# A weight tile's low part made in pieces of 256 columns on GpSimd instead of one of up to 1024

## The chip, the cores and the metric

The kernel runs on one core of a Trainium2 chip. The metric is the device time of one execution in microseconds; lower is better. The engines are named as in the profile: PE multiplies matrices (PEld are its weight loads), DVE, ACT and POOL (GpSimd) work elementwise, SP issues the transfers.

## What is computed

Two layers of a decoder over 1024 tokens of width 1024. In each, three groups of attention heads run side by side on the same normed input; then come a SwiGLU network and a gated embedding.

```python
for i in range(DEPTH):                      # DEPTH = 2
    proj = rms_norm(h, attn_norm[i]) @ w_in[i]          # 1024 x 2664
    # 6 heads: softmax attention from two low-rank projections (mla_w_uq, mla_w_ukv)
    # 5 heads: softmax over the 256 keys that an indexer scores highest, for each query
    # 5 heads: stick-breaking attention (cumulated log-sigmoids)
    h = h + mix @ w_o[i]
    hf = rms_norm(h, ffn_norm[i])
    h = h + (silu(hf @ w_gate[i]) * (hf @ w_up[i])) @ w_down[i]     # width 2816
    g = sigmoid(rms_norm(h, ple_norm[i]) @ w_ple_gate[i])
    h = h + g * (p[i] @ w_ple_proj[i])
return rms_norm(h, final_norm)
```

## The kernel before

The residual is held features by tokens, in two halves of 512 tokens. The program runs a dense part (in-projection, output projection, SwiGLU, embedding) of one half while the attention of another half runs beside it: `weave` mixes the two streams in one order for PE, which is written out by hand. On the other engines a scheduler with a model of durations orders what is ready.

**The weights.** To keep the accuracy of float32, each weight tile is split in two parts of a shorter type. `load_cols` fetches a tile of 128 rows, `kt` k tiles and some columns (mostly 8 k tiles of 128 columns, or 4 of 256 for `w_down`: 1024 columns a partition) into `wr`, which has three buffers. `split_w` copies it on ACT into the high part `wh` (L185) and subtracts that from it on POOL into the low part `wl` (L186). `wh` and `wl` have two buffers each. `gemm` then runs three matmuls for each k tile: high weights with the high and the low activations (L256, L257), low weights with the high ones (L258). For one of the weights (`mla_w_ukv`) columns change places, and the split goes k tile by k tile, in pieces of 256 columns.

**Others on POOL.** L881 multiplies the two factors of the stick-breaking weights, which PE then transposes (L818). L609 scales the gate of the SwiGLU. L313 adds up squares for the norms.

**Others on DVE.** The norms make the low part of the scaled activations (L302). The SwiGLU has L608 on the gate and L623 for the low part of the product, L572 adds the down projection. Queries are split at L750, keys and values at L283. L826 makes the low part of the transposed attention weights from PSUM; L878 is the scan of the stick-breaking heads. The 256 highest keys are found by a bit search that runs in the background of the attention: for each of 31 bits it makes a candidate (`cand`, L1084), counts the scores above it with one operation for each of two or four query tiles (`junk`, L1072), and then takes the bit or not (`inc`, L1086, and `key`, L1087), each of the three on 2 or 4 columns. `inc`, `key` and the next `cand` depend on each other in this order.

```python
            DVE.scalar_tensor_tensor(cand, key, 1 << b, xm, op0=ALU.bitwise_or, op1=ALU.bitwise_xor)
            yield from count(cand.bitcast(F32), ALU.is_ge)
            DVE.tensor_scalar(inc, cnt, float(TOPK), float(1 << b), op0=ALU.is_ge, op1=ALU.mult)
            DVE.tensor_tensor(key, key, inc, op=ALU.bitwise_or)
```

Of the kernel before, what the change touches and what calls it, by code (L numbers as in the profile page):

```python
# [13 lines left out]
ALU = mybir.AluOpType  # L14
AX = mybir.AxisListType

T = 1024
# [9 lines left out]
TOPK = 256  # L27
# [17 lines left out]
CUT = 3  # L45
VAL_AT = 6
# [12 lines left out]
def f32(ap):  # L59
    return ap.bitcast(F32)  # L60


def weave(main, side, main_total, side_total, finished, clock):
    """Traces a part of two streams together: side advances with main, at the pace that gets it through side_total
    as main ends, and in any case until finished(). Each yields what its piece weighs; side yields None while it
    waits for something that main has yet to trace."""
# [21 lines left out]
def trunk(ctx: ExitStack, tc, x, p, w_in, attn_norm, mla_q_norm, mla_w_uq, mla_kv_norm, mla_w_ukv,  # L88
# [35 lines left out]
    def spare_tile(m):  # L124
        """Where attention had tiles that it no longer needs."""
# [15 lines left out]
    # ---------------------------------------------------------------- constants  # L141
# [33 lines left out]
    # ---------------------------------------------------------------- the residual's first half  # L175
    # ---------------------------------------------------------------- helpers of the dense part
    def split_w(raw, hi, lo, *order):
        """Parts of raw; order: the views of a k tile between which its columns change places."""
        if order:
            read, write = order  # L180
            parts = [(read(raw[:, k]), write(hi[:, k]), write(lo[:, k])) for k in range(raw.shape[1])]
        else:
            parts = [(raw, hi, lo)]
        for a, h, l in parts:
            ACT.copy(h, a)  # L185
            POOL.tensor_tensor(l, a, f32(h), op=ALU.subtract)  # L186
        return hi, lo

    def load_cols(segs, kt, *order):
        """Weight columns as [128 (k), kt, sum of widths], split in two float32r parts."""  # L190
# [45 lines left out]
    def after(n, f):  # L236
        """TensorE's part of something, once n more k tiles' products have been traced."""
# [11 lines left out]
    def gemm(ps, w, act, ks, m0=0, first=True, last=True):  # L249
        """ps[m, tokens] (+)= w^T act over the k tiles ks, in three passes that keep float32's accuracy."""  # L250
# [12 lines left out]
    def gemm_pair(x, y, act, ks, cut):  # L263
        """Two products; the first one's last k tile comes after some of the second one's."""
# [9 lines left out]
    def priority(by):  # L274
        """Ahead (by < 0) or behind in the order in which free engines pick what is ready."""
# [9 lines left out]
    class Norm:  # L285
        """rms_norm over n feature tiles that come one at a time, as float32r parts of src * gain in res; what they
# [1003 lines left out]
```

## Time and profile before

| | |
|---|---|
| time, median of 3 runs | 3304.84 us (3303.76 to 3309.46) |
| span of the profiled execution | 3305.8 us, 1.0 us over the median |
| mean granted clock of PE | 0.978 of 2.4 GHz |
| PE busy | 3101.8 us, 94% |
| DVE busy | 2404.7 us, 73% |
| ACT busy | 1484.6 us, 45% |
| POOL busy | 1378.0 us, 42%, of it 1046.1 in L186 |
| transfers | 363.50 MB, mean 110 GB/s |

The first table of the profile gives the busy time of each engine. A view by stretches of the span gives the same for parts of it, with the granted clock. The chain that ended last is followed back from the last instruction, at each step to what released it or to the one before it on its engine; its shares say whose time the end hangs on. The views by line give count, busy time, mean duration, and what ended the idle time before. A timeline has the instructions in order of time.

### The profile page before, as it was taken

The numbers are of one execution on the slowest core, as the hardware profiler recorded it, in microseconds if no ns is written. First come the engines' busy times: TensorE is split into PE (matmuls) and PEld (weight loads), VectorE is DVE, ScalarE is ACT, GpSimd is POOL, SyncE is SP. The second block draws the span as 40 slices with busy tenths as digits, with TensorE's granted clock in tenths as the row PEclk, the third lists the DMA queues.
The fourth block names the chain that finished last, engine by engine and source line by source line (L and its number), as shares of the span: only waits on it lengthen the run. The fifth ranks groups of instructions, "written<-read, shape, count | busy, mean of one in ns | idle before, by whom it ended". The sixth has DMA issues, their size and how long they took to land.

```text
span 3305.8 us, 42153 instructions
## 1 busy us (share of the span) xinstructions
PE 3101.8 (94%) x15059; PEld 2566.7 (78%) x15059; DVE 2404.7 (73%) x3829; ACT 1484.6 (45%) x2485; POOL 1378.0 (42%) x712
## 2 busy tenths in 40 slices
PE   8889999988998999999999999879999999999998
PEld 6667888777787888877788787767787887788886
DVE  5978667799998646798865646899998665444445
ACT  4544654444445545444444434534444455322224
POOL 3332244444333332544344543444333343455444
PEclk9999999999999999999999999989999999999999
DMA  7464463222233345433333355422233223333332
GB/s 196 112 183 122 149 177 96 89 81 89 84 93 93 107 113 161 143 99 95 99 107 95 99 155 160 137 61 86 90 93 97 87 79 111 106 96 96 96 93 74
DMA packets 549937, 363.50 MB, mean 110 GB/s; under 512 B 134671, under 2 KB 491743, under 8 KB 549727
## 3 DMA queue, kind: packets, MB, share of 16 engines
q1 hardware_dynamic: 549727, 360.81, 37.4%
q8 instruction: 119, 1.95, 0.2%
q14 instruction: 91, 0.75, 0.1%
HBM read 310.65 MB, written 50.08 MB: 109 GB/s over the span
## 4 chain that ended last, share of the span: by engine, by line
PE 59%; DVE 30%; issue 4%; ACT 3%; DMA 2%; POOL 1%; SPq 0%; DVEq 0%; ACTq 0%; POOLq 0%
PE D L256 16%; PE D L257 16%; PE D L258 16%; DVE junk L1072 7%; PE S L778 5%; DVE A L878 3%; PE O L835 3%; DVE PT L826 2%; PE T L818 2%; DVE inc L1086 2%; DVE act L302 1%; DVE cand L1084 1%; DVE h L572 1%; DVE key L1087 1%; DVE qh L750 1%
## 5 line engine op out<-in xcount | busy, mean ns | idle before, releaser
L186 POOL TENSOR_TENSOR wl<-wr,wh 128x1024 fp32r<-128x1024 f32 (+2 forms) x456 | 1046.1, 2295 | 1488.1 <-ACT wh L185 1401.1
L256 PE MATMUL D<-act,wh 128*128 128x512 f32 x3416 | 1372.2, 402 | 53.0 <-DVE h L572 18.3
L258 PE MATMUL D<-act,wl 128*128 128x512 f32 x3416 | 1347.3, 394 | 7.3 <-POOL wl L186 7.3
L257 PE MATMUL D<-act,wh 128*128 128x512 f32 x3416 | 1347.9, 395 | 2.4 <-DVE act L623 2.1
L256 PEld LDWEIGHTS D<-act,wh 128*128 128x128 f32 x3416 | 651.2, 191 | 200.9 <-issue 16.4
L258 PEld LDWEIGHTS D<-act,wl 128*128 128x128 f32 x3416 | 649.5, 190 | 154.2 <-POOL wl L186 12.0
L257 PEld LDWEIGHTS D<-act,wh 128*128 128x128 f32 x3416 | 651.4, 191 | 128.2 <-DVE act L623 3.2
L185 ACT CAST wh<-wr 128x1024 fp32r<-128x1024 f32 (+2 forms) x456 | 452.2, 994 | 634.6 <-PE D L257 335.9
L1072 DVE TENSOR_SCALAR_CACHE_REDUCE junk<-isc,cand 128x512 uint8<-128x512 f32 (+5 forms) x396 | 372.0, 939 | 6.1
L826 DVE TENSOR_TENSOR PT<-T,PT 128x384 fp32r<-128x384 f32 (+1 forms) x320 | 201.7, 630 | 110.7 <-ACT PT L825 109.9
L835 PE MATMUL O<-PT,V 128*128 128x256 f32 x1280 | 221.2, 291 | 57.8 <-DVE PT L826 53.3
L835 PEld LDWEIGHTS O<-PT,V 128*128 128x128 f32 x1280 | 198.4, 193 | 95.8 <-DVE PT L826 66.3
L825 ACT CAST PT<-T 128x384 fp32r<-128x384 f32 (+1 forms) x320 | 173.4, 542 | 177.5 <-PE T L818 169.6
L881 POOL TENSOR_TENSOR P<-P,A 128x127 f32<-128x127 f32 (+3 forms) x80 | 102.3, 1282 | 268.6 <-DVE A L878 114.9
L778 PE MATMUL S<-kh,qh 128*128 128x384 f32 (+4 forms) x544 | 208.1, 384 | 0.9 <-ACT P L864 0.7
L778 PE MATMUL S<-kl,qh 128*128 128x384 f32 (+4 forms) x544 | 205.5, 378 | 2.9 <-DVE kl L283 2.8
L818 PE MATMUL T<-identF,P 128*128 128x128 f32 x1152 | 185.2, 280 | 16.0 <-POOL P L881 10.0
L609 POOL TENSOR_TENSOR tmp<-tmp,rr 128x512 f32<-128x512 f32 x88 | 116.8, 1327 | 113.9 <-DVE tmp L608 97.8
L608 DVE SCALAR_TENSOR_TENSOR tmp<-tmp 128x512 f32<-128x512 f32 x88 | 136.6, 1552 | 34.9 <-ACT tmp L607 34.7
L623 DVE TENSOR_TENSOR act<-tmp,act 128x512 fp32r<-128x512 f32 x88 | 136.7, 1553 | 33.6 <-ACT act L622 33.6
L1038 DVE SCALAR_TENSOR_TENSOR isc<-P,iw,isc 128x384 f32<-128x384 f32 (+2 forms) x84 | 113.2, 1350 | 59.9 <-ACT P L1032 59.4
L818 PEld LDWEIGHTS T<-identF,P 128*128 128x128 f32 x1152 | 137.4, 144 | 20.2 <-POOL P L881 12.3
(217 smaller groups left out, 3412.8 us busy)
## 6 DMA issues: line engine op xcount, KB each, us to landing
wr<-in_w_gate_dram SPq DMA_DIRECT2D x88, 512.0 KB, 3.8
wr<-in_w_up_dram SPq DMA_DIRECT2D x88, 512.0 KB, 3.8
wr<-in_w_down_dram SPq DMA_DIRECT2D x80, 512.0 KB, 3.5
wr<-in_w_in_dram SPq DMA_DIRECT2D x44, 512.0 KB, 4.0
wr<-in_w_in_dram SPq DMA_DIRECT2D x76, 256.0 KB, 3.7
wr<-in_w_o_dram SPq DMA_DIRECT2D x32, 512.0 KB, 4.2
wr<-in_w_ple_gate_dram SPq DMA_DIRECT2D x32, 512.0 KB, 3.8
h<-h SPq DMA_DIRECT2D x56, 256.0 KB, 4.3
```

Source lines behind the costliest of these rows:

```text
L185: ACT.copy(h, a)
L186: POOL.tensor_tensor(l, a, f32(h), op=ALU.subtract)
L256: PE.matmul(ps, a, ah, start=first and i == 0, stop=False)
L257: PE.matmul(ps, a, al, start=False, stop=False)
L258: PE.matmul(ps, b, ah, start=False, stop=last and i == len(ks) - 1)
L623: DVE.tensor_sub(lo, t, f32(hi))
L778: PE.matmul(o, a, b, start=j == 0, stop=j == len(mms) - 1)
L818: PE.transpose(ps[:, o:o + 128], self.P[q][:, j * 128:(j + 1) * 128], identF)
L825: ACT.copy(pt[:, 0, o:], self.ps[:, o:])
L826: DVE.tensor_sub(pt[:, 1, o:], self.ps[:, o:], f32(pt[:, 0, o:]))
L835: PE.matmul(self.O[:, :256], self.head.V[:, j, :], pt[:, s, o:o + 256], start=j == 0 and s == 0, stop=j == 2 * self.n - 1 and s == 1)
L1072: DVE.tensor_scalar(junk[:, :n], isc[:, off[t]:off[t] + n], c[:, i:i + 1], None, op0=op, op1=ALU.add, accum_out=cnt[:, i:i + 1])
```

## The change

The high part is still made by one copy on ACT. The subtraction is issued in pieces of `PIECE // columns` k tiles: two k tiles of 128 columns, or one of 256. A tile of 1024 columns becomes four instructions, one of 768 three, one of 832 four of 208, and the 512 columns of `w_ple_proj` two. The tiles that are split k tile by k tile stay as they were. The rest of the diff removes comments, so that lines behind `split_w` stand 10 further down (L186 becomes L196, L258 L268, L881 L891).

```diff
--- before.py
+++ after.py
@@ -43,6 +43,7 @@
 WR, WH, WL, ACTS, TMPS, MIXS = 3, 2, 2, 26, 3, 2
 FASTEST = 0.3
 CUT = 3
+PIECE = 256
...
     def split_w(raw, hi, lo, *order):
...
         if order:
             read, write = order
-            parts = [(read(raw[:, k]), write(hi[:, k]), write(lo[:, k])) for k in range(raw.shape[1])]
+            for k in range(raw.shape[1]):
+                a, h, l = read(raw[:, k]), write(hi[:, k]), write(lo[:, k])
+                ACT.copy(h, a)
+                POOL.tensor_tensor(l, a, f32(h), op=ALU.subtract)
+            return hi, lo
+        ACT.copy(hi, raw)
+        if len(raw.shape) == 2:
+            views = [t.rearrange("p (k c) -> p k c", k=2) for t in (raw, hi, lo)]
         else:
-            parts = [(raw, hi, lo)]
-        for a, h, l in parts:
-            ACT.copy(h, a)
-            POOL.tensor_tensor(l, a, f32(h), op=ALU.subtract)
+            views = raw, hi, lo
+        a, h, l = views
+        n = max(PIECE // a.shape[2], 1)
+        for k in range(0, a.shape[1], n):
+            ks = slice(k, min(k + n, a.shape[1]))
+            POOL.tensor_tensor(l[:, ks], a[:, ks], f32(h[:, ks]), op=ALU.subtract)
         return hi, lo
```

On POOL, in the attention of the first half, before:

```order
L186 TENSOR_TENSOR wl_1303<-wr_1300,wh_1302 128x1024
L881 TENSOR_TENSOR P_1192<-P_1192,A_1193 128x511
L186 TENSOR_TENSOR wl_1389<-wr_1386,wh_1388 128x1024
L881 TENSOR_TENSOR P_1279<-P_1279,A_1280 128x127
L881 TENSOR_TENSOR P_1279<-P_1279,A_1280 128x255
L881 TENSOR_TENSOR P_1354<-P_1354,A_1355 128x383
```

and now (`wl` is the low part, `P` and `A` the stick-breaking factors):

```order
L196 TENSOR_TENSOR wl_1348<-wr_1345,wh_1347 128x256 x4
L891 TENSOR_TENSOR P_1234<-P_1234,A_1235 128x511
L196 TENSOR_TENSOR wl_1437<-wr_1434,wh_1436 128x256 x4
L891 TENSOR_TENSOR P_1324<-P_1324,A_1325 128x127
L891 TENSOR_TENSOR P_1324<-P_1324,A_1325 128x255
L891 TENSOR_TENSOR P_1402<-P_1402,A_1403 128x383
```

Four pieces stand where one subtraction stood, in one row as they follow each other without another wait; L881 keeps its places around them.

On PE, at the first products of a `w_down` tile of four k tiles of 256 columns, with the engines that an instruction waits for in brackets, before:

```order
L256 MATMUL D_6339<-act_5684,wh_6335 128x512
L257 MATMUL D_6339<-act_5685,wh_6335 128x512
L258 MATMUL D_6339<-act_5684,wl_6336 128x512 [waits Pool_49]
L256 MATMUL D_6339<-act_5959,wh_6335 128x512
L257 MATMUL D_6339<-act_5960,wh_6335 128x512
L258 MATMUL D_6339<-act_5959,wl_6336 128x512
L256 MATMUL D_6339<-act_6059,wh_6335 128x512
L257 MATMUL D_6339<-act_6060,wh_6335 128x512
L258 MATMUL D_6339<-act_6059,wl_6336 128x512
```

and now:

```order
L266 MATMUL D_6570<-act_5876,wh_6563 128x512
L267 MATMUL D_6570<-act_5877,wh_6563 128x512
L268 MATMUL D_6570<-act_5876,wl_6564 128x512 [waits Pool_49]
L266 MATMUL D_6570<-act_6169,wh_6563 128x512
L267 MATMUL D_6570<-act_6170,wh_6563 128x512
L268 MATMUL D_6570<-act_6169,wl_6564 128x512 [waits Pool_49]
L266 MATMUL D_6570<-act_6275,wh_6563 128x512
L267 MATMUL D_6570<-act_6276,wh_6563 128x512
L268 MATMUL D_6570<-act_6275,wl_6564 128x512 [waits Pool_49]
```

The instructions are the same and in the same order; where the first use of the low part waited for the whole tile, each k tile's first use now waits for its own piece.

## Rows read from the trace of the kernel before

**Rows 1.** The page's first table: busy time, share of the span, instructions.

```profile
PE 3101.8 (94%) x15059; PEld 2566.7 (78%) x15059; DVE 2404.7 (73%) x3829; ACT 1484.6 (45%) x2485; POOL 1378.0 (42%) x712
```

**Rows 2.** Busy time by stretches of the span. Columns: stretch, its length, then busy us and instructions of PE, PEld, DVE, ACT and POOL, granted clock, share of the DMA engines, GB/s.

```profile
0.00:300.00 300.00, 259.64 (x1220) 206.21 (x1220) 226.49 (x496) 141.78 (x285) 101.74 (x71) 0.95 0.57 157
...
600.00:900.00 300.00, 266.07 (x1299) 219.89 (x1298) 289.55 (x436) 134.44 (x198) 135.91 (x67) 0.96 0.29 86
...
2100.00:2400.00 300.00, 256.72 (x1248) 212.02 (x1247) 287.80 (x457) 136.62 (x203) 131.26 (x67) 0.94 0.27 80
...
2700.00:3000.00 300.00, 288.88 (x1343) 238.46 (x1342) 164.06 (x213) 121.40 (x183) 144.89 (x73) 0.98 0.34 101
```

**Rows 3.** The chain that ended last: shares of the span by engine and by line on the page, and by line with a decimal from the view of the chain (cut at its end there).

```profile
PE 59%; DVE 30%; issue 4%; ACT 3%; DMA 2%; POOL 1%; SPq 0%; DVEq 0%; ACTq 0%; POOLq 0%
...
PE D L256 16%; PE D L257 16%; PE D L258 16%; DVE junk L1072 7%; PE S L778 5%; DVE A L878 3%; PE O L835 3%; DVE PT L826 2%; PE T L818 2%; DVE inc L1086 2%; DVE act L302 1%; DVE cand L1084 1%; DVE h L572 1%; DVE key L1087 1%; DVE qh L750 1%
...
by line: PE D L256 16.2%; PE D L257 15.9%; PE D L258 15.8%; DVE junk L1072 7.1%; PE S L778 4.7%; issue 4.3%; DVE A L878 2.7%; PE O L835 2.5%; DVE PT L826 2.5%; PE T L818 2.2%; DVE inc L1086 1.5%; DVE act L302 1.5%; DVE cand L1084 1.2%; DVE 
```

**Rows 4.** POOL's subtractions: the group of the 1024-column ones (count | busy us, mean ns | idle us before), and all that write `wl`, with the shortest, median and longest in ns.

```profile
L186 POOL TENSOR_TENSOR wl<-wr,wh 128x1024 fp32r<-128x1024 f32 x400 | 974.0, 2435 | 1339.5 <-ACT wh L185 1258.1 <-PE T L818 24.9 <-PE S L778 13.0
...
L186 POOL TENSOR_TENSOR wl<-wr,wh x456: 726/2395/3447, 12.1 to 3274.2; 128x1024 fp32r<-128x1024 f32 x132, 128x256 fp32r<-128x256 f32 x8, 128x512 fp32r<-128x512 f32 x8, 128x768 fp32r<-128x768 f32 x4
```

**Rows 5.** DVE's operations: first by line, with the shortest, median and longest duration in ns and the time of the first and last start; then by line and shape, with count | busy us, mean ns | idle us before.

```profile
L1086 DVE TENSOR_SCALAR inc<-cnt x124: 134/169/2364, 113.3 to 2471.8; 128x2 int32<-128x2 f32 x62, 128x4 int32<-128x4 f32 x62
...
L1087 DVE TENSOR_TENSOR key<-key,inc x124: 127/161/2357, 113.4 to 2472.7; 128x2 int32<-128x2 int32 x62, 128x4 int32<-128x4 int32 x62
...
L1084 DVE SCALAR_TENSOR_TENSOR cand<-key,xm x124: 129/161/2391, 111.4 to 2464.4; 128x2 int32<-128x2 int32 x62, 128x4 int32<-128x4 int32 x62
...
L302 DVE SCALAR_TENSOR_TENSOR act<-h,gall,act x100: 735/752/2778, 9.9 to 2730.5; 128x512 fp32r<-128x512 f32 x100
...
L608 DVE SCALAR_TENSOR_TENSOR tmp<-tmp x88: 674/1372/2827, 520.8 to 3210.8; 128x512 f32<-128x512 f32 x88
...
L750 DVE TENSOR_TENSOR qh<-qraw,qh x72: 689/690/2854, 46.0 to 2685.6; 64x512 fp32r<-64x512 f32 x72
...
L1072 DVE TENSOR_SCALAR_CACHE_REDUCE junk<-isc,cand x396: 585/933/1281, 108.9 to 2480.7; 128x384 uint8<-128x384 f32 x66, 128x640 uint8<-128x640 f32 x66, 128x896 uint8<-128x896 f32 x66
...
L826 DVE TENSOR_TENSOR PT<-T,PT x320: 529/677/693, 127.6 to 2788.7; 128x512 fp32r<-128x512 f32 x96, 128x384 fp32r<-128x384 f32 x64
...
L608 DVE SCALAR_TENSOR_TENSOR tmp<-tmp 128x512 f32<-128x512 f32 x88 | 136.6, 1552 | 34.9 <-ACT tmp L607 34.7
...
L302 DVE SCALAR_TENSOR_TENSOR act<-h,gall,act 128x512 fp32r<-128x512 f32 x100 | 128.4, 1291 | 26.0 <-ACT act L301 25.4
...
L750 DVE TENSOR_TENSOR qh<-qraw,qh 64x512 fp32r<-64x512 f32 x72 | 72.2, 1003 | 23.3 <-ACT qh L749 21.2
...
L1086 DVE TENSOR_SCALAR inc<-cnt 128x2 int32<-128x2 f32 x62 | 43.5, 702 | 0.7
...
L1086 DVE TENSOR_SCALAR inc<-cnt 128x4 int32<-128x4 f32 x62 | 33.8, 544 | 0.4
```

**Rows 6.** Two short timelines, POOL's rows and then DVE's of each: start us, us, engine, line and operation.

```profile
148.21 2.38 POOL L186 TENSOR_TENSOR wl<-wr,wh 128x1024 fp32r<-128x1024 f32 x1 [3.84 <-ACT wh L185]
...
148.26 2.35 DVE L1086 TENSOR_SCALAR inc<-cnt 128x2 int32<-128x2 f32 x1
...
724.23 2.68 POOL L609 TENSOR_TENSOR tmp<-tmp,rr 128x512 f32<-128x512 f32 x1 [0.63 <-DVE tmp L608]
726.87 1.54 POOL L881 TENSOR_TENSOR P<-P,A 128x767 f32<-128x767 f32 x1
728.38 2.38 POOL L186 TENSOR_TENSOR wl<-wr,wh 128x1024 fp32r<-128x1024 f32 x1
...
725.74 1.20 DVE L1086 TENSOR_SCALAR inc<-cnt 128x4 int32<-128x4 f32 x1
726.97 1.46 DVE L1087 TENSOR_TENSOR key<-key,inc 128x4 int32<-128x4 int32 x1
728.47 2.31 DVE L1084 SCALAR_TENSOR_TENSOR cand<-key,xm 128x4 int32<-128x4 int32 x1
```

**Rows 7.** Timelines at the pieces of 256 columns that the kernel already has (x2 are two of them, one behind the other): POOL's row and DVE's at 189 us, and POOL's at 2045 us.

```profile
189.38 1.44 POOL L186 TENSOR_TENSOR wl<-wr,wh 128x256 fp32r<-128x256 f32 x2
...
189.28 0.16 DVE L1086 TENSOR_SCALAR inc<-cnt 128x2 int32<-128x2 f32 x1
189.47 0.66 DVE L1087 TENSOR_TENSOR key<-key,inc 128x2 int32<-128x2 int32 x1
190.17 0.66 DVE L1084 SCALAR_TENSOR_TENSOR cand<-key,xm 128x2 int32<-128x2 int32 x1
...
2045.52 1.45 POOL L186 TENSOR_TENSOR wl<-wr,wh 128x256 fp32r<-128x256 f32 x2 [4.08 <-ACT wh L185]
```

**Rows 8.** Waits for POOL and of POOL: who waited for whom, us in total, times, longest us.

```profile
POOL wl L186 <- ACT wh L185: 1401.1, 357, 14.9
...
PE D L258 <- POOL wl L186: 7.3, 8, 2.5
...
PE T L818 <- POOL P L881: 10.0, 2, 5.2
...
ACT wh L185 <- POOL tmp L609: 83.8, 23, 3.9
```

## The prediction

> **What bounds the kernel now.** I read the page's first line and the granted clock by stretch first [rows 1, 2], then the chain that ended last [rows 3], then the durations of the operations on DVE and POOL [rows 4, 5], then two short timelines [rows 6, 7], and at the end who waits for POOL [rows 8]. PE is busy for 3101.8 of 3305.8 us, and its granted clock is near the upper level of 2.4 GHz nearly everywhere. From 2700 to 3000 us PE is the limit: busy for 96%, at a clock of 0.98. From 600 to 900 and from 2100 to 2400 us it is not. There DVE is busy for 289.6 and 287.8 of 300 us, PE idles for 34 and 43 us, and its clock falls to 0.96 and 0.94 [rows 2]. The chain says the same: over the span PE holds 59% of it and DVE 30% [rows 3], so DVE's time on the chain is about 990 us.
>
> What is odd in DVE's rows is the distance of the longest from the shortest duration of one shape [rows 5]. `inc`, an operation on 2 or 4 columns, takes 0.13 us at least and 2.36 us at most; `key` and `cand` are like it; L302 takes 0.735 to 2.78 us, L608 0.67 to 2.83. The counting operation L1072, which is longer than these, has no such tail: at most 1.28 us, its largest shape. The timelines show what the long ones do. At 148.21 us POOL starts a 1024-column subtraction; `inc` starts at 148.26 and takes 2.35 us, to the moment when POOL is done [rows 6, 4]. So some DVE operations can't run beside a POOL subtraction. They wait for its end, and the profile shows the wait as busy time. L826, which reads PSUM, and L1072 do not wait [rows 5].
>
> How much is that? With the shortest duration taken as the true one [rows 5], L302 loses (1291 - 735) ns x 100 = 56 us in its largest group, L608 (1552 - 674) x 88 = 77 us, `inc` (702 - 134) x 62 + (544 - 134) x 62 = 61, L750 (1003 - 689) x 72 = 23. These four alone are 217 us of DVE's 2404.7.
>
> **The change, part by part.** *Removed and added on POOL.* 400 subtractions of 1024 columns at 2.435 us become 1600 of 256. Two subtractions of 256 columns back to back, at the places where the old code already has them, take 1.44 and 1.45 us [rows 7], 0.72 us each, so four take 2.88 us, 0.45 more than one. That is 400 x 0.45 = 180 us; 48 smaller tiles, divided in two to four, add under 15 by the same two rows. POOL goes from 1378 to some 1570 us, 47% of the span. As most of its idle time is waiting for ACT's copy (1401.1 us, 357 times) [rows 8], the added time lies in that idle time and costs nothing by itself. What covers it is that a weight tile of eight k tiles serves 24 matmuls; where PE is the limit it runs 1343 instructions in 300 us [rows 2], 0.22 us each, so a tile lasts PE 5.4 us, against 2.9 on POOL.
>
> *The order.* PE's instructions stand as before, and of POOL's groups one pair has changed places; the pieces of a tile stand together, nothing gets between them. On ACT and DVE some ten places differ by a neighbour or two, on SP some thirty transfers move by a place or two. I cost that at nothing, with 5 us either way in the range: the longest wait on one neighbour in the rows, a transpose for L881, is 5.2 us [rows 8].
>
> *Waits of PE.* With pieces, a matmul of L258 waits for the piece that holds its k tile; about 1100 matmuls more have a wait than before. Where a piece is done long before, the bound is what PE waits for POOL's low parts now, 7.3 us in 8 places [rows 8]. The first piece is ready 1.7 us earlier than the whole tile was (2.4 - 0.7), the last 0.45 us later but needed 4 us later (18 matmuls), so this can give back a few microseconds and cost few. I take zero.
>
> *What DVE gains.* An operation that waits singly meets a POOL operation of 0.72 us in place of 2.4: the wait falls to about 30%. But POOL is in such an operation for a larger share of the time (by 2.88/2.4, a fifth), and an operation that follows directly meets the next piece. At 189.28 us stands what will be the rule: two halves of 256 columns, `inc` passes before them, `key` waits 0.66 us for the first half, goes between the halves, and `cand` waits 0.66 us for the second [rows 7]. The trio `inc`, `key`, `cand` depend on each other and come together, so a tile in four pieces can hold all three up, for 0.36 + 0.7 + 0.7 us, where one long subtraction holds up the first for 1.2 us on average and lets the others pass. For the trio I leave 75% of the wait, for single operations 40%.
>
> *What of it lies on the path.* By the chain [rows 3], `inc` holds 1.5% of the span, 50 us. All 124 of them at 0.169 us would be 21, so at least 29 us are wait. `cand` has 1.2%, 40 us, of it at least 20 wait; `key` 1%, 33 us, at least 13. The trio has 62 us. L302 has 1.5%, 50 us; 44% of its busy time is wait (1291 against 735 ns), 22 us. L750 has 1%, 33 us, a third of it wait: 10 us. L608 and others like it stand below the rows shown, each with less than L750's share; three or four of them could have 0 to 40 us of wait, and I take 20. Singles: 52 us. Of these waits those behind weight tiles are a part, as the 1024-column subtractions are 974 of POOL's 1378 us [rows 1, 4]: 71%. So the trio saves 62 x 0.71 x 0.25 = 11 us, the singles 52 x 0.71 x 0.6 = 22 us. Sum: 33 us on the chain.
>
> *What is late next.* Where DVE stops being last, PE is. It has 34 and 43 us of idle time in the two stretches, and 40 in the first, where the bit search begins [rows 2], so there is room for 33 us, but the saved time is not all in those places. I take nine tenths, **30 us**. Bounds: nothing at the one end. At the other all that could be saved if pieces meet nobody twice: (62 + 52 + 20) x 0.71 x 0.7 = 67 us, the further 20 being L608 and its like at their most. The profiled execution has a span of 3305.8 us, 1.0 us over the median of the three runs (3304.84), so the median should fall to 3304.8 - 30 = 3275 us.
>
> **A rule that speaks against it.** The rows show DVE getting in at the seam of two POOL operations with no gap between them: at 726.9 us `inc` gets in between L609 and L881 and `key` starts only then; at 728.4 `key` gets in between L881 and a weight tile, and `cand` waits for the tile [rows 6]. And no maximum lies further than 2.4 us over its minimum [rows 5], as it would if a waiting operation had to sit out a second subtraction. The Trainium skill, GPSIMD Engine Reference, Instruction dispatch, says that consecutive POOL instructions are no barrier between its cores: each core starts the next as soon as its own share of the one before is done. By that rule pieces without a wait between them might never let go of what DVE needs. The halves at 189.38 stand against it, but the second of those has a wait of its own on ACT, which the later pieces of a tile will not have. It is the second rival.
>
> **The rivals.**
> *PE hides it.* The 33 us lie where PE has work in reserve, and the order in which PE must take its instructions makes the next wait end just as late. For it: PE has 94% and its stalls are spread over many small waits. Against: DVE is busy for 96% of two stretches, which nothing but less DVE work can shorten. It gives 0 to 6 us, about 3302.
>
> *The pieces hold as one.* If DVE can't get in between pieces of one tile, a waiting operation faces 2.88 us in place of 2.4, and a fifth more often. The waits behind weight tiles on the chain, 114 x 0.71 = 81 us, grow by 2.88/2.4 squared, 1.44: 36 us more, **3341**. It decides from about half: if DVE gets in at fewer than 52% of the seams, 33 x share no longer covers 36 x (1 - share). For it: no wait between the pieces. Against: every seam in the timelines.
>
> *POOL runs late.* Each time DVE gets in between pieces, POOL waits for DVE's operation (a subtraction took 3.45 us at most, against 2.40 in the middle) [rows 4]; with three seams and 0.7 us at each a tile can end 2 us later. Behind it in POOL's queue stand L881, for which PE's transposes wait (10.0 us now), and L609, and ACT's next copy waits for POOL: 83.8 us now [rows 8]. If a third of a microsecond were lost for each of the 80 L881, the cost is 27 us and the sum is near zero, 3302; this and the first rival look alike in the time and differ in the waits.
>
> *The change does nothing.* The instruction stream has the pieces, so this is out.
>
> **How the numbers follow.** A measurement of this kernel tells 0.2%, 6.6 us, from no change: faster is below 3298, slower above 3311. The forecast (15 to 70 us saved) has 0.72; PE hiding it or POOL running late together 0.17, of it 0.14 within 0.2%, 0.01 faster and 0.02 slower; the pieces as one 0.08; a disturbed order 0.03, a third each way. Faster 0.74, same 0.15, slower 0.11. The range: the low end takes 65 us off, close to the upper bound of what could be saved (67): 3240. The high end lies at no change and 4 us over: 3309. About 1 in 10 is left above and 1 in 10 below.
>
> **What would show it.** In the profile of the changed kernel `inc`, `key`, `cand`, L302 and L608 should have maxima near 0.7 us over their minima where only weight tiles are in the way; L608 should come down to a mean near 0.95 us, DVE's busy time by some 200 us to about 2200. POOL should be at 1530 to 1620 us. DVE's busy share between 600 and 900 us should fall little, as the work moves forward, while PE's idle time there falls from 34 to about 25 us. The trio should show more waits, shorter ones. If maxima of 2.9 us remain on these lines, the pieces hold as one and the time goes up. If the waits fall as said and the span stays, PE or POOL took it: then PE's waits for L881 or for DVE's PSUM readers must have grown.

## The result and the profile after

The changed kernel takes 3230.15 us (median of four runs, 3227.67 to 3231.06). Before, on the same chip, it was 3304.30 us (3303.59 to 3309.46). The ratio on record is 0.9765, with a 95% interval from 0.9753 to 0.9776; the quotient of the two medians is 0.9776, at the end of this interval. It is 74 us less, where 30 were forecast with 65 as the far end. The direction and the mechanism were right, the size was not. The profiled execution has a span of 3229.2 us, 76.6 less than before.

The page's first table of the changed kernel, as in [rows 1]:

```profile
PE 3075.5 (95%) x15059; PEld 2553.0 (79%) x15059; DVE 2131.9 (66%) x3829; ACT 1485.9 (46%) x2485; POOL 1723.2 (53%) x1980
```

DVE lost 273 us of busy time (some 200 were forecast) and POOL gained 345 (180 to 195 were forecast). PE runs the same 15059 matmuls in 26.3 us less. Its idle time, span less busy time, went from 204.0 to 153.7 us. 26.3 and 50.3 are the whole 76.6.

Busy time by stretches after, columns as in [rows 2]:

```profile
0.00:300.00 300.00, 267.36 (x1275) 213.31 (x1276) 220.40 (x522) 146.49 (x296) 126.44 (x171) 0.97 0.60 162
600.00:900.00 300.00, 276.08 (x1381) 229.24 (x1380) 292.49 (x484) 143.72 (x215) 163.81 (x176) 0.98 0.30 91
2100.00:2400.00 300.00, 274.98 (x1401) 228.91 (x1401) 287.97 (x510) 140.76 (x218) 155.09 (x165) 0.97 0.29 88
2700.00:3000.00 300.00, 294.38 (x1327) 242.22 (x1326) 99.16 (x154) 97.39 (x130) 191.91 (x228) 0.99 0.35 107
```

In the two stretches where DVE is the limit it is as full as before, but gets through more: 484 and 510 instructions instead of 436 and 457. PE gets through 1381 and 1401 matmuls instead of 1299 and 1248 [rows 2]. Its idle time there fell from 34 to 24 and from 43 to 25 us, and its granted clock rose from 0.96 to 0.98 and from 0.94 to 0.97 (the upper of its levels, 2.4 GHz, being 1). The changed kernel is further on at the same time, so these stretches do not hold quite the same work.

DVE's operations after, by line with the shortest, median and longest duration in ns, and two of them by shape with the mean. The lines of before are ten lower, and the rows are in the order of [rows 5]:

```profile
L1096 DVE TENSOR_SCALAR inc<-cnt x124: 133/169/1194, 109.6 to 2404.7; 128x2 int32<-128x2 f32 x62, 128x4 int32<-128x4 f32 x62
...
L1097 DVE TENSOR_TENSOR key<-key,inc x124: 130/168/1462, 109.8 to 2405.4; 128x2 int32<-128x2 int32 x62, 128x4 int32<-128x4 int32 x62
...
L1094 DVE SCALAR_TENSOR_TENSOR cand<-key,xm x124: 129/164/1865, 107.8 to 2397.3; 128x2 int32<-128x2 int32 x62, 128x4 int32<-128x4 int32 x62
...
L312 DVE SCALAR_TENSOR_TENSOR act<-h,gall,act x100: 736/755/2372, 10.3 to 2661.3; 128x512 fp32r<-128x512 f32 x100
...
L618 DVE SCALAR_TENSOR_TENSOR tmp<-tmp x88: 674/808/1253, 505.0 to 3134.9; 128x512 f32<-128x512 f32 x88
...
L1082 DVE TENSOR_SCALAR_CACHE_REDUCE junk<-isc,cand x396: 587/934/1281, 105.2 to 2413.6; 128x384 uint8<-128x384 f32 x66, 128x640 uint8<-128x640 f32 x66, 128x896 uint8<-128x896 f32 x66
...
L312 DVE SCALAR_TENSOR_TENSOR act<-h,gall,act 128x512 fp32r<-128x512 f32 x100 | 97.4, 980 | 29.1 <-ACT act L311 28.6
L618 DVE SCALAR_TENSOR_TENSOR tmp<-tmp 128x512 f32<-128x512 f32 x88 | 74.0, 841 | 36.3 <-ACT tmp L617 36.1
```

The shortest durations stay, the longest fall by 0.4 to 1.6 us. The 40 waits of more than 0.7 us that are left all lie behind the other POOL operations, which were not divided. The gate's L618 has a mean of 841 ns instead of 1552. L1082, which never waited, is unchanged. Summed over all DVE operations (each one's duration over the usual short one of its line and shape, which 5% of them undercut, where the difference is more than 0.12 us), the waits went from 514 us in 418 operations to 229 us in 507: more waits, shorter ones. That they are waits for POOL can be seen in the kernel before: 414 of the 418 end within 0.3 us of the end of a POOL operation.

Timelines of the changed kernel at 143 us, POOL's row and then DVE's (x4: four pieces, one behind the other):

```profile
143.85 2.82 POOL L196 TENSOR_TENSOR wl<-wr,wh 128x256 fp32r<-128x256 f32 x4 [3.85 <-ACT wh L187]
...
143.90 0.71 DVE L1096 TENSOR_SCALAR inc<-cnt 128x2 int32<-128x2 f32 x1
144.52 0.15 DVE L351 SCALAR_TENSOR_TENSOR rtmp<-rtmp,ms 128x4 f32<-128x4 f32 x1
144.64 0.65 DVE L1097 TENSOR_TENSOR key<-key,inc 128x2 int32<-128x2 int32 x1
145.22 0.15 DVE L352 SCALAR_TENSOR_TENSOR rstd<-rtmp,rstd 128x4 f32<-128x4 f32 x1
145.33 0.65 DVE L1094 SCALAR_TENSOR_TENSOR cand<-key,xm 128x2 int32<-128x2 int32 x1
```

This is the case in [rows 6], 148 us, with pieces: `inc` waits for the first, `key` for the second, `cand` for the third, with a small operation slipping through in between. The three wait for 1.6 us together, where `inc` alone waited for 2.2.

POOL after, by shape and by line (as [rows 4]), and then waits (as [rows 8]):

```profile
L196 POOL TENSOR_TENSOR wl<-wr,wh 128x256 fp32r<-128x256 f32 x1668 | 1363.6, 849 | 1175.4 <-ACT wh L187 1138.9 <-PE T L828 26.4 <-DMA kraw<-kr 6.1
...
L196 POOL TENSOR_TENSOR wl<-wr,wh x1684: 624/741/2350, 12.6 to 3200.1; 128x256 fp32r<-128x256 f32 x187, 128x208 fp32r<-128x208 f32 x1
```

```profile
POOL wl L196 <- ACT wh L187: 1147.3, 352, 13.5
...
PE D L268 <- POOL wl L196: 3.7, 4, 1.8
...
PE T L828 <- POOL P L891: 6.6, 2, 3.9
...
PE O L845 <- DVE PT L836: 35.4, 21, 5.0
```

A piece takes 0.74 us at the median, as estimated, but 0.85 on average, since pieces wait for DVE as DVE waits for them (the timeline at the end of this document shows such a piece). POOL is still idle for 1147 us waiting for ACT, and PE's waits for POOL are no longer than before. PE's wait for `PT` by DVE, its largest, was 53.3 us:

```profile
PE O L835 <- DVE PT L826: 53.3, 33, 7.0
```

This subtraction itself never waits for POOL [rows 5, L826]. It stands behind operations in DVE's queue that do.

### The profile page after: what moved, and what is told of

The parts are those of the page before. It is cut to its first block, busy times and chain, and to the rows that moved or that the text cites. A ratio compares the mean times of both kernels' runs of the same rounds, so it can differ in the third digit from the quotient of the medians.

```text
span 3229.2 us, 43704 instructions
## 1 busy us (share of the span) xinstructions
PE 3075.5 (95%) x15059; PEld 2553.0 (79%) x15059; DVE 2131.9 (66%) x3829; ACT 1485.9 (46%) x2485; POOL 1723.2 (53%) x1980
## 5 line engine op out<-in xcount | busy, mean ns | idle before, releaser
L196 POOL TENSOR_TENSOR wl<-wr,wh 128x256 fp32r<-128x256 f32 x1684 | 1374.2, 847 | 1183.8 <-ACT wh L187 1147.3
L268 PE MATMUL D<-act,wl 128*128 128x512 f32 x3416 | 1342.6, 393 | 3.8 <-POOL wl L196 3.7
L268 PEld LDWEIGHTS D<-act,wl 128*128 128x128 f32 x3416 | 646.8, 189 | 148.0 <-POOL wl L196 6.4
L187 ACT CAST wh<-wr 128x1024 fp32r<-128x1024 f32 (+3 forms) x432 | 443.7, 1027 | 683.0 <-PE D L267 533.4
L1082 DVE TENSOR_SCALAR_CACHE_REDUCE junk<-isc,cand 128x512 uint8<-128x512 f32 (+5 forms) x396 | 371.9, 939 | 6.1
L891 POOL TENSOR_TENSOR P<-P,A 128x127 f32<-128x127 f32 (+3 forms) x80 | 101.2, 1268 | 206.6 <-DVE A L888 110.6
L1048 DVE SCALAR_TENSOR_TENSOR isc<-P,iw,isc 128x384 f32<-128x384 f32 (+2 forms) x84 | 97.4, 1161 | 79.6 <-ACT P L1042 79.5
L630 DVE SCALAR_TENSOR_TENSOR tmp<-tmp,D 128x512 f32<-128x512 f32 x88 | 60.2, 684 | 107.8 <-POOL tmp L619 80.8
L853 ACT COPY o<-O 64x256 f32<-64x256 f32 x128 | 47.4, 370 | 174.9 <-PE O L845 173.4
```

The costliest lines, as they stand in the source:

```text
L187: ACT.copy(hi, raw)
L196: POOL.tensor_tensor(l[:, ks], a[:, ks], f32(h[:, ks]), op=ALU.subtract)
L268: PE.matmul(ps, b, ah, start=False, stop=last and i == len(ks) - 1)
L1082: DVE.tensor_scalar(junk[:, :n], isc[:, off[t]:off[t] + n], c[:, i:i + 1], None, op0=op, op1=ALU.add, accum_out=cnt[:, i:i + 1])
```

## The experiments

Times are medians. "Waits" is the sum of DVE's waits worked out as above, "searches" the length of the five stretches from the first to the last count of a bit search, added up. All ratios are those on record, to the kernel before on the same chip, whose median was 3304 to 3308 us there; they differ from the quotients of the medians by up to 0.001.

| kernel | us | ratio, interval | waits us | searches us | PE idle us | clock | POOL busy us |
|---|---|---|---|---|---|---|---|
| before | 3304.3 | 1 | 514 | 1119 | 204 | 0.978 | 1378 |
| after (256) | 3230.2 | 0.9765 [0.9753, 0.9776] | 229 | 1067 | 154 | 0.986 | 1723 |
| p512 | 3275.6 | 0.9897 [0.9881, 0.9914] | 375 | 1106 | 180 | 0.979 | 1522 |
| rev | 3228.4 | 0.9756 [0.974, 0.9773] | 234 | 1071 | 151 | 0.986 | 1720 |
| nosub | 3152.7 | 0.9529 [0.9514, 0.9543] | 53 | 1020 | 104 | 0.993 | 299 |
| p128 | 3218.6 | 0.9728 [0.9714, 0.9743] | 175 | 1063 | 143 | 0.987 | 2030 |
| inside | 3253.4 | 0.984 [0.9826, 0.9853] | 447 | 1069 | 167 | 0.984 | 1476 |
| outside | 3284.1 | 0.9931 [0.9917, 0.9944] | 299 | 1123 | 188 | 0.977 | 1627 |
| dupkey | 3246.2 | 0.9818 [0.9805, 0.9832] | 247 | 1105 | 158 | 0.980 | 1724 |
| dup3 | 3295.8 | 0.9961 [0.9946, 0.9977] | 285 | 1200 | 190 | 0.979 | 1731 |
| allp | 3213.8 | 0.9716 [0.9703, 0.973] | 162 | 1052 | 138 | 0.984 | 2092 |
| p64 | 3320.4 | 1.0044 [1.0029, 1.0059] | 273 | 1096 | 208 | 0.975 | 2594 |
| nt_whole | 3223.7 | 0.9749 [0.9735, 0.9764] | 436 | 1031 | 149 | 0.986 | 1375 |
| nt_piece | 3172.2 | 0.9592 [0.9576, 0.9608] | 165 | 1008 | 117 | 0.989 | 1729 |

**What makes the gain.** Theory A is the prediction's: DVE's waits for the end of a POOL subtraction. Theory B: PE has the first k tile's low part earlier. Theory C: neighbours that changed places on ACT and DVE.

*p512*, pieces of 512 columns:

```diff
-PIECE = 256
+PIECE = 512
```

> Pieces of 512 columns instead of 256. The theory that DVE's waits for the end of a subtraction set the gain (theory A): the gain follows the length of what DVE waits for, 2.40 us whole, 1.44 us estimated for 512 columns (two pieces of 0.72), 0.72 for 256; the step from 2.40 to 1.44 is 57% of the step from 2.40 to 0.72, so 42 of the 74 us, about 3262 us, with DVE's long waits (over 0.12 us) near 340 us in total, between 515 and 232. The theory that PE's earlier first piece makes the gain (theory B): the first piece is there 0.96 us earlier than the whole tile instead of 1.68, which gives about the same 3262, so this run sizes the gain and does not tell A from B. The theory that it is the places of some ten instructions that changed on ACT and DVE (theory C): any time, 3230 as likely as 3304.

It saves 32 us, DVE's waits fall by 139. The gain follows the length of the pieces, at three quarters of what the proportion with the estimated 1.44 us would give. A piece of 512 columns takes 1.30 us at the median, and by that it is two thirds:

```profile
L196 POOL TENSOR_TENSOR wl<-wr,wh x848: 723/1296/2748, 12.0 to 3244.2; 128x512 fp32r<-128x512 f32 x164, 128x256 fp32r<-128x256 f32 x4, 128x416 fp32r<-128x416 f32 x2
```

The clock stays at 0.979, and PE's busy time falls by 7 us only, so most of these 32 us were saved without a faster PE.

*rev*, the pieces in reverse order:

```diff
-        for k in range(0, a.shape[1], n):
+        for k in reversed(range(0, a.shape[1], n)):
```

> The pieces of 256 columns in reverse order, the last k tiles first, so that PE, which begins with k tile 0, must wait for all of the pieces at its first use of the low part, as it did before the change. Theory A: nothing that DVE meets is changed, 3230 us within 10 either way. Theory B: the gain goes and the tile, which now ends 0.45 us later than one instruction, costs a little, 3300 to 3320. Theory C: between, as the order is disturbed once more.

3228.4 us: nothing is lost when PE has to wait for the last piece first. Theory B falls. Of theory C it takes a part as well: some places on POOL, ACT and DVE differ from the changed kernel's order, and the time is the same. p512 speaks against it too, as POOL's operations stand there in the order of before, by their names, and 32 us are saved all the same. Theory C was not tested by itself.

*nosub*, no subtraction:

```diff
...
-        for k in range(0, a.shape[1], n):
-            ks = slice(k, min(k + n, a.shape[1]))
-            POOL.tensor_tensor(l[:, ks], a[:, ks], f32(h[:, ks]), op=ALU.subtract)
-        return hi, lo
+        return hi, hi
...
```

> Leaves out the low part of the weights: no subtraction on GpSimd, and the third matmul of each k tile takes the high part again, so that PE's work and ACT's copies stay and the output is less exact. It shows what is left of the waits behind weight tiles. Theory A: of the 232 us of DVE waits in the changed kernel some 160 lie behind weight tiles; if a bit less than half of a wait comes out in the time, as it did so far (74 us of 283), 40 to 60 us more are to be had, 3170 to 3190. Theory B: PE waits for no subtraction at all, but it waits for few now (3.7 us), so the time is within 10 us of 3230, unless the lock is what counts.

77 us more than the pieces give, which is more than the 40 to 60 expected, for 176 us of wait less. It frees POOL for its other work too, so not all of it need be DVE's. The whole price of the subtractions on POOL was some 155 us, of which pieces of 256 columns save half.

*p128*, pieces of 128 columns (a k tile of `w_down` in two):

```diff
-PIECE = 256
+PIECE = 128
...
-            POOL.tensor_tensor(l[:, ks], a[:, ks], f32(h[:, ks]), op=ALU.subtract)
+            for c in range(0, a.shape[2], PIECE):
+                cs = slice(c, min(c + PIECE, a.shape[2]))
+                POOL.tensor_tensor(l[:, ks, cs], a[:, ks, cs], f32(h[:, ks, cs]), op=ALU.subtract)
```

> Pieces of 128 columns (of a w_down tile half a k tile each), 8 instructions for a tile. No row has a piece of 128 columns; from 0.72 us for 256 and 2.40 for 1024 (0.56 us more for 256 columns more) it should take about 0.44. Theory A: DVE waits for 0.44 instead of 0.72 us, the step is a sixth of the one that gave 74 us, 12 us more, about 3218; POOL grows by 400 x (8 x 0.44 - 2.88) = 256 us and stays under 65% of the span. The rival that POOL then runs late: each tile ends 0.6 us later plus the seams that DVE takes, and the time comes back to 3230 to 3260, with PE's and ACT's waits for POOL grown.

3218.6 us, as theory A had it. A piece takes 0.46 us at the median (the shortest below, 0.40 us, has only 104 columns) and 0.54 on average; POOL's 2030 us still hide.

```profile
L198 POOL TENSOR_TENSOR wl<-wr,wh x3368: 402/463/2532, 12.4 to 3186.1; 128x128 fp32r<-128x128 f32 x198, 128x104 fp32r<-128x104 f32 x1
...
L198 POOL TENSOR_TENSOR wl<-wr,wh 128x128 fp32r<-128x128 f32 x3336 | 1672.7, 539 | 927.5 <-ACT wh L187 890.2 <-PE T L830 20.9 <-DMA kraw<-kr 5.8
```

**Where the gain lies.** *inside* and *outside* divide the tiles by their place: those that POOL makes while a bit search runs, and the others. One run has pieces for the first, the other for the second. The 135 and 313 of the expectations are 129 and 319 in the traces: the ranges below also count six pieces of tiles that are split k tile by k tile and stay as they were.

```diff
+SEARCH = ((15, 29), (33, 40), (89, 131), (192, 224), (303, 343))
...
-        n = max(PIECE // a.shape[2], 1)
+        piece = PIECE if any(p <= at < q for p, q in SEARCH) else 1024
+        n = max(piece // a.shape[2], 1)
```

> One part of the change alone: pieces of 256 columns only for the 135 of 448 tiles that GpSimd makes while a bit search runs (the five stretches of L1072 in the trace of before), one instruction for all others. The theory that the waits count where the search makes DVE the limit: the five stretches fell from 1119 to 1068 us with the change, so some 50 of the 74 us come from here, about 3255. The rival that each tile gives alike: 30% of 74, 22 us, about 3283.

> The other part alone: pieces only for the 313 tiles outside the bit searches. If the search is where the waits count: some 25 of the 74 us, about 3280. If each tile gives alike: 52 us, about 3253. With the run on the inside: if the two savings together come to 74 within some 10, the parts add up.

The savings are 54 and 24 us, together 78: the parts add up, and 54 of the 78 come from the 29% of the tiles that meet a search. The waits fell by 66 us in the run on the inside and by 214 in the one on the outside. So a microsecond of wait taken away was worth 0.8 us on average at the searches and 0.1 elsewhere. The stretches from 600 to 900 us show it, first of inside and then of outside:

```profile
600.00:900.00 300.00, 274.99 (x1374) 228.53 (x1373) 292.27 (x473) 140.94 (x210) 164.78 (x166) 0.98 0.29 88
```

```profile
600.00:900.00 300.00, 268.00 (x1302) 221.70 (x1301) 288.86 (x447) 134.75 (x199) 140.41 (x79) 0.95 0.28 86
```

With pieces in the search alone PE runs 1374 matmuls in this stretch, almost as many as the 1381 of the changed kernel; with pieces everywhere else 1302, as before.

**What a microsecond of the search's chain costs.** *dupkey* and *dup3* issue `key` once and three times more in each step.

```diff
                 DVE.tensor_tensor(key, key, inc, op=ALU.bitwise_or)
+                DVE.tensor_tensor(key, key, inc, op=ALU.bitwise_or)
```

> The changed kernel with the last small operation of each step of the bit search, key (or with inc), issued twice; the second changes nothing. 124 operations more of 0.16 us and, with the mean wait that key has now (31 us in 124), up to 0.41 us: 20 to 51 us of DVE's time more. If the search's chain is the limit wherever it runs, this comes out in the span one for one, 3250 to 3281, and TensorE's clock falls with it, a few us more. If TensorE's reserve hides a part, as the prediction assumed with its nine tenths and its idle time, a part; if it hides it all, 3230 to 3235.

> The changed kernel with key issued four times in each step, 372 operations more; the copies change nothing. With one copy the five searches took 37 us longer and the span 15 to 16. Three copies should lengthen the searches by some 111 us. If TensorE's reserve takes a fixed amount of it (the 21 us that were missing with one copy): 3230 + 111 - 21 = 3320. If it takes a share everywhere: 3230 + 3 x 16 = 3278. If the operation is only as dear as its waits, three in a row pass in one gap between pieces, and the searches lengthen by less: 372 x 0.16 = 60 us and 3255 to 3290.

The searches take 37 and 133 us longer, the kernel 16 and 66: 0.43 and 0.49 of it, a share and no fixed amount (the first is rough, as 16 us is taken between two chips whose medians of before differ by 3.5 us). So even where DVE is busy for 96% half of a longer chain is made up for elsewhere. I had expected 60 or 111 us more of searching from three copies; it was 133, 0.36 us for each copy. The copies have means of 0.30 to 0.37 us, like `key` in the changed kernel (0.39 and 0.42), so copies in a row do not pass in one gap.

**The trio's part.** *nt_whole* and *nt_piece* leave the trio out, one with whole tiles, one with pieces:

```diff
-                DVE.scalar_tensor_tensor(cand, key, 1 << b, xm, op0=ALU.bitwise_or, op1=ALU.bitwise_xor)
                 yield from count(cand.bitcast(F32), ALU.is_ge)
-                DVE.tensor_scalar(inc, cnt, float(TOPK), float(1 << b), op0=ALU.is_ge, op1=ALU.mult)
-                DVE.tensor_tensor(key, key, inc, op=ALU.bitwise_or)
...
-            DVE.tensor_tensor(cand, key, xm, op=ALU.bitwise_xor)
+            DVE.tensor_tensor(cand, key, key, op=ALU.bitwise_xor)
```

> Leaves out the three small operations of each step of the bit search (inc, key, cand: the bits of the threshold are never set, so the sparse heads keep other keys); the counts stay. Weight tiles whole, as before the change. It is one half of a pair; the difference to nt_piece is what the pieces are worth when the trio isn't there to wait. The trio's 185 us of busy time go, at most that much less than 3305, and at least the 60 us that it would take without any wait: 3120 to 3245.

> The other half of the pair: the trio left out, weight tiles in pieces of 256 columns. The theory that the trio's waits are the larger part of the gain (its waits behind weight tiles fell from 105 to 57 us inside the searches, and there a microsecond of wait is a microsecond of time): 48 of the 76 us can't be saved any more, the pair differs by 22 to 35 us. The sizes that the prediction gave (the trio a third of the saving, other operations two thirds): the pair differs by about 50 us.

The pair differs by 51 us, so my theory that the trio's waits are the larger part falls, and the prediction's division, a third for the trio, stands as far as this can tell. It can't tell it cleanly. With whole tiles and no trio, the other operations inside the searches wait for 79 us behind subtractions, where they waited for 31 with the trio. The gate's L618 has now a mean of 1784 ns instead of 1552:

```profile
L618 DVE SCALAR_TENSOR_TENSOR tmp<-tmp 128x512 f32<-128x512 f32 x88 | 157.0, 1784 | 38.6 <-ACT tmp L617 38.4
```

Who comes next on DVE while POOL subtracts has to wait; take it away and the next one does.

**A better version, and the end of it.** *allp* has pieces of 128 columns for the weights and of 256 for POOL's other operations:

```diff
...
-                        POOL.tensor_tensor(t, t, ffn.rep, op=ALU.mult)
+                        for c in range(0, HALF, 256):
+                            cs = slice(c, c + 256)
+                            POOL.tensor_tensor(t[:, cs], t[:, cs], ffn.rep[:, cs], op=ALU.mult)
...
-                POOL.tensor_tensor(P[:, :n - 1], P[:, :n - 1], A[:, 1:n], op=ALU.mult)
+                for c in range(0, n - 1, 256):
+                    e = min(c + 256, n - 1)
+                    POOL.tensor_tensor(P[:, c:e], P[:, c:e], A[:, c + 1:e + 1], op=ALU.mult)
```

> Pieces of 128 columns for the weights, and the other GpSimd operations of 512 to 1023 columns (the gate's product, the sum of squares, the product of P and A) in pieces of 256 as well. Behind those lie some 60 us of the 175 that DVE still waits with pieces of 128. Waits on DVE set the gain: 25 to 30 us less of them, at 0.26 us of time for each us of wait as from before to after, 6 to 8 us, about 3211. The rival: these results are wanted by TensorE and ACT as a whole and now come 0.1 to 0.5 us later: 3219 to 3230.

3213.8 us is the lowest time of a kernel that does all the work, 94 us under before. Over p128 it is 5 us, and the intervals overlap: the other operations are worth little.

*p64*, pieces of 64 columns (the diff is against p128):

```diff
-PIECE = 128
+PIECE = 64
```

> Pieces of 64 columns, 16 for a tile. The shortest durations are 0.40 us for 128, 0.72 for 256, 1.29 for 512 columns, so one of 64 should take 0.25 at least, 4.0 us for a tile against 3.2 with 128. If shorter waits still pay: DVE waits for 0.25 instead of 0.40 us, a seventh of the step that gave 74 us and so at most 8 us more than the 3219 of pieces of 128, about 3212. If the tile's own length begins to count (with DVE getting in at fifteen seams of each): POOL near 75% of the span, PE and ACT wait for it, 3230 to 3300.

3320.4 us is slower than before and above both ranges that were expected. Two things go wrong at once, and what each of them costs was not separated.

The first is that POOL runs late. A piece takes 0.33 us at the median, and never under 0.30 with the full 64 columns, where 0.25 had been worked out as the least. With 0.38 on average a tile of 16 pieces takes 6.0 us (with 128 columns 4.3), and the prediction's own estimate of what a tile lasts PE is 5.4 us. POOL is busy for 2594 us, ACT waits for low parts before its next copy, and PE waits for low parts and for a transpose's input again. The lengths of p64's pieces, and waits:

```profile
L198 POOL TENSOR_TENSOR wl<-wr,wh x6736: 259/326/2378, 12.7 to 3300.5; 128x64 fp32r<-128x64 f32 x199
...
L198 POOL TENSOR_TENSOR wl<-wr,wh 128x64 fp32r<-128x64 f32 x6704 | 2242.1, 377 | 581.8 <-ACT wh L187 581.2
...
ACT wh L187 <- POOL wl L198: 99.4, 50, 4.1
PE T L343 <- DVE rr L325: 23.0, 7, 6.0
PE D L270 <- POOL wl L198: 19.5, 25, 2.4
PE T L830 <- POOL P L893: 16.2, 4, 7.3
```

With pieces of 128 columns these four waits are 36.0, 6.5, 4.4 and 7.6 us.

The second is that DVE no longer gets in at every seam. A timeline of p64, DVE's row and then POOL's (x14: fourteen pieces, one behind the other):

```profile
2839.85 6.03 DVE L314 SCALAR_TENSOR_TENSOR act<-A,gall,act 128x512 fp32r<-128x512 f32 x1 [0.93 <-ACT act L313]
```

```profile
2838.77 1.32 POOL L325 TENSOR_TENSOR rr<-rr,tmp 128x512 f32<-128x512 f32 x1
2840.03 4.00 POOL L198 TENSOR_TENSOR wl<-wr,wh 128x64 fp32r<-128x64 f32 x14
2843.95 1.31 POOL L325 TENSOR_TENSOR rr<-rr,tmp 128x512 f32<-128x512 f32 x1
```

L314 starts in the middle of a sum of squares, sits out its end, fourteen pieces and the next sum, and runs when that is over. Of some 400 waits in this kernel 72 go on past two or more ends of POOL operations, up to 15, and these alone make up 182 us. With pieces of 128 columns one wait of some 570 does, with 256 columns none of 507, with whole tiles none of 418. (A wait past a single end proves less: 15 of the 507 can be counted so, but each of these had started less than 0.1 us before the end that it passed.) The waits that had gone from 514 to 175 us rise to 273.

## Why the prediction was right in direction and too small

**The reading of what binds was right.** DVE's long durations are waits for POOL, they fall with the length of POOL's instruction (514, 375, 229, 175 and 53 us of wait with 1024, 512, 256, 128 columns and none), and the time falls with them. The operations' minima, the gate's mean (841 ns, where 950 was written), PE's idle time from 600 to 900 us (24 us, where 25 was written) and more, shorter waits of the trio came as the last part of the prediction said. DVE's busy share there didn't fall at all, 97.5 against 96.5%.

**What was costed at nothing cost nothing.** PE's waits on the pieces: rev. The order: rev again, whose interval overlaps the changed kernel's. POOL's added time was mis-sized, 345 us against 180 to 195: the 0.72 us for a piece left out that POOL now waits for DVE as well (0.85 on average). It hides all the same, in waiting for ACT.

**The step that failed is "What of it lies on the path".** It took each line's share of the chain and subtracted the time that all 124 operations of the line would take without a wait. But not all of them lie on the chain. Counted one by one, 84 of the `inc` do, for 49.7 us, and 84 times 0.134 us is 11: 38 us are wait, where the prediction had 29, written as "at least" and then added up as the size. Counted in this way (on the chain of before, the duration of each operation over the usual short one of its shape), the trio has 92 us of wait where 62 were taken. The singles and everything below the rows shown (L623, L283, L608, L1103, L1038 and more) have 106 where 52 were taken. This miss is another one: L302 and L750 have about 34 of the 106, close to the 32 taken, and some 70 stand in lines that no row showed, for which the prediction put 20. Together that is 198 instead of 114. Of it 143 us, 72%, lie behind 1024-column tiles; the 71% of the prediction were right.

**The shares left were too high, a smaller error of the same sign.** Behind weight tiles the trio's waits went from 107 to 57 us, so 53% stay, where 75% were taken; the other operations' from 342 to 104, 31% instead of 40%. The overlap that was counted against the trio, that all three meet pieces, is real (the timeline at 143 us) but not the rule. Neither share had been worked out from rows: the example beside the 75%, 0.36 + 0.7 + 0.7 us for 1.2, would even have lengthened the trio's wait. And the shares measured here are of all waits. The chain of the changed kernel can be followed back for the last 14% of its span only, so what stayed on it was not counted.

With the counted sizes the prediction's own sum reads 92 x 0.72 x 0.47 = 31 for the trio and 106 x 0.72 x 0.69 = 53 for the others, 84 us, and nine tenths of it 75. That it meets the measured 74 is worked out afterwards and no proof of each factor. What the runs support of it is the division (by the pair without the trio 25 and 51 us, with the reservation made there). The upper bound rested on the same count: 198 x 0.72 x 0.7 would have been 100 us instead of 67, and the range would have held the time.

**TensorE's clock had no term.** PE's 15059 matmuls took 26.3 us less at 0.986 than at 0.978. In every run its busy time times the clock is within 0.4% of 3030 us, so the difference is the clock's. It rose most where PE's idle time fell most, from 2100 to 2400 us (0.94 to 0.97, with 18 us less idle time). Whether these 26 us are to be counted beside the waits or are one way in which the shorter waits come out is not shown. p512 saved 32 us with 7 us less of PE's busy time, and dupkey's 16 us are 11 of PE's busy time and 4 of its idle time.

**The rivals.** *PE hides it* is true for the larger part of the waits: outside the searches 214 us of wait less were worth 24. It is not true at the searches, where the prediction had argued that it isn't. *The pieces hold as one* is false for 256 columns and becomes true in part for 64. The Trainium skill's warning (GPSIMD Engine Reference, Instruction dispatch) that consecutive POOL instructions are no barrier between its cores fits what p64 shows; that its mechanism is the cause is not shown. For 256 columns the measurement decides against the conclusion that I drew from it. *POOL runs late* is false for 256 (PE's wait for `P` fell from 10.0 to 6.6 us) and also comes true with 64. ACT's wait for POOL behind the gate's product, the 83.8 us named in this rival, fell to 2.9:

```profile
ACT wh L187 <- POOL tmp L619: 2.9, 3, 1.2
```

**What stays open.** How the 54 us inside the searches divide. The trio's waits there fell by 48 us and the other operations' own by 14; at half a microsecond of time for each of chain, as dupkey and dup3 price it, this is some 30 us. That price may be too low here: it was measured by lengthening the search, and in the run on the inside the searches are 50 us shorter and the kernel 54, nearly one for one. If it holds, the other 24 could be operations that never wait for POOL themselves but stand behind the trio in DVE's queue. PE's wait for such a one, `PT`, fell from 53.3 to 37.6 us in the run on the inside, and only to 50.7 in the one on the outside:

```profile
PE O L851 <- DVE PT L842: 37.6, 24, 4.3
```

```profile
PE O L851 <- DVE PT L842: 50.7, 29, 6.5
```

That is consistent with it, and was not tested by itself.

## What to carry to other kernels

Where one engine's long instruction keeps another engine waiting, its length is a price paid by whoever comes next, and cutting it costs only that engine's own time as long as that has cover and the one that waits gets in between the pieces. Count what a wait is worth operation by operation along the chain, and not as a line's share less the time of all its operations; and ask by stretch, since the same microsecond was worth 0.8 us at the searches and 0.1 elsewhere. Don't take the smallest piece: 128 columns was the best size tried, and 64 was worse than not cutting at all.

## What I had not expected of the hardware

DVE gets in at the seams between POOL's instructions with pieces of 1024, 512 and 256 columns, and with 128 all but once, but not with 64. POOL's durations there are 2.40, 1.30, 0.74, 0.46 and 0.33 us at the median. With 64 columns 72 of some 400 waits went on past two ends or more, at the worst for 5.3 us and fifteen ends. Whether it is the length of the instructions or how densely they follow each other was not separated. Between the last two sizes a kernel that was 2.7% faster became 0.4% slower.

Waiting goes both ways: a POOL piece of 0.74 us at the median took up to 2.35 us. This longest one is the second of the two here (POOL's row, then DVE's), and it ends 0.5 us after DVE's scans do:

```profile
1485.19 3.50 POOL L196 TENSOR_TENSOR wl<-wr,wh 128x256 fp32r<-128x256 f32 x2
...
1486.64 1.52 DVE L888 TENSOR_TENSOR_SCAN A<-A,zeros 128x256 f32<-128x256 f32 x2
```

378 pieces of the changed kernel take more than 0.9 us, and 375 of them end 0.5 to 0.8 us after a DVE operation does.
